# Values of three retention heads by seven products instead of eight

## The chip, the cores and the metric

The kernel runs on one core of a Trainium2 chip. The metric is the time of one execution on the device in microseconds (us). Engines go by the names of the profile: PE is TensorE's matmul, PEld its weight load, DVE is VectorE, ACT is ScalarE, POOL is GpSimd, SP is SyncE.

## The reference, cut to what matters

A trunk of two decoder layers over 512 tokens of 1024 channels, all in float32. Each layer has a half-step SwiGLU, a token mixer, a second half-step SwiGLU and a gated embedding. The mixer of the first layer is a retention with 4 heads; the change is in its input projections.

```python
def retention(h, w_in, gn_w, w_out):
    B, S, _ = h.shape                       # 1, 512 tokens
    H, DK, DV, C = RET_HEADS, RET_DK, RET_DV, RET_CHUNK     # 4, 256, 512, 128
    q, k, v, g = jnp.split(h @ w_in, [H * DK, 2 * H * DK, 2 * H * DK + H * DV], axis=-1)
    pos = jnp.arange(S, dtype=jnp.float32)
    q = rotary(q.reshape(B, S, H, DK), pos)
    k = rotary(k.reshape(B, S, H, DK), pos) * (DK ** -0.5)
    v = v.reshape(B, S, H, DV)
...
    y = jax.nn.silu(g) * o.reshape(B, S, H * DV)
    return y @ w_out
```

The values `v` are, for each head, a product of 512 tokens x 1024 channels with 1024 x 512 weights.

## The kernel before, in words

**Precision.** A float32 product is made of three products of rounded parts: each operand is split into a high part (a cast to float32r on ACT, line 88 or 134) and a low part (what the cast lost). `Weights.split` (line 86) makes the low part on DVE (line 89). `Weights.negated` makes it without DVE: ACT casts (134) and writes the negative (135), and a DMA from POOL's queue (136) reads the weights from memory once more and adds them to that negative. Pairs marked `direct` are split, the others negated.

**Seven products.** Most projections are by the Strassen-Winograd scheme: a weight block of 1024 x 256 is a `Pair` of two tensors, `q` (blocks a11 and a22) and `r` (a12 and a21). The activations' side has fixed forms (`b11`, `b22`, `b21`, `t1` to `t4`), each held as high and low part in `unit_a` to `unit_d`; the weights' side needs four sums (`sums`, line 168, on DVE), each split again into the tiles `s12` and `s34`, and the parts of a12 in the tile `a12`; the profile calls these `s` and `a`. The blocks of `q` are split in a large tile `w8`, which the profile calls `w`. `Strassen.begin` multiplies the first three products (36 matmuls of 256 columns) into two banks of PSUM, `g` and `u`, and adds across the banks (L597 to L601); `rest` does the other four (48 matmuls); `join` the last additions (L621 to L623).

**The retention's projections.** Queries and keys of heads 1, 2, 3, 0 and six gates are 14 such pairs (`ret_order`), numbered 0 to 13: 2 and 3 are head 2, 4 and 5 head 3, 6 and 7 head 0, 8 to 13 gates. The loop begins pair i + 1, then does the rest of pair i, then `finished(i)` (joins and, for a query or key, six DVE instructions of the rotary). The values of a head are plain products: `values` takes four weight chunks of 1024 columns (`ret_v`), and streams them in 96 matmuls of 512 columns with the activations as stationary operand into four banks, one for each 128 tokens (L871 to L873); ACT evicts them (L876) and POOL stores them (L877). Head 1's come ahead of the loop; `RET_V = {1: 2, 4: 3, 7: 0}` puts head 2's behind the rest of pair 1, head 3's behind pair 4, head 0's behind pair 7.

**What sets the order.** PE runs in the order in which the code is written. A scheduler sets the order on DVE, ACT, POOL and SP; each engine then works strictly in its order. `W.plan` is the order in which weights are loaded by SP into four `wraw` tiles, and `take` prepares tiles two entries ahead. There are three `w8` tiles, three each of `s12` and `s34`, two of `a12`, seven `tmp`, eight banks, each used in turn. `next_sums(behind)` makes the sums of the pair after next, ordered behind a DVE instruction.

Of the kernel before, what the change touches and what calls it, by code (L numbers as in the profile page):

```python
# [27 lines left out]
LOOKAHEAD = 2  # L28
RET_V = {1: 2, 4: 3, 7: 0}
KEPT = 7  # L30
# [27 lines left out]
class Weights:  # L58
# [149 lines left out]

    def next_sums(self, behind):
        self.pairs_used += 1  # L210
        if self.held:
            with self.tc.issue_after(behind.ins):
                self.held()
            self.held = None
        self.behind = (behind,)
        self.emit_sums()
        self.behind = ()
# [3 lines left out]
def trunk(ctx, tc, a):  # L221
# [24 lines left out]
    for i in range(4):  # L246
# [6 lines left out]
        ffn_src.append((ins, outs))  # L253
    ret_v = [[a["ret_v"][h][:, c * 1024 : (c + 1) * 1024] for c in range(4)] for h in range(RH)]
    ret_g = [[a["ret_g"][c] for c in range(4)]]
    at = {"q": 0, "k": 4, "0": 8, "1": 9}
    ret_pairs = []
    for kind, hd in ret_order:
        i = at[kind] + (hd if kind in "qk" else 2 * (hd - 1))
        ret_pairs.append(Pair(4, a["ret_p"][i, 0], a["ret_p"][i, 1]))  # L260
    for i in [0, 1] + [i + 2 for i in RET_V]:
        ret_pairs[i].direct = True
# [20 lines left out]
    plan_ffn(0)  # L283
    W.plan += ret_v[1] + ret_pairs[0:1]
    for i in range(len(ret_pairs)):
        W.plan += ret_pairs[i + 1 : i + 2]
        if i in RET_V:
            W.plan += ret_v[RET_V[i]]
    W.plan += ret_g[0] + ret_o[0] + ret_o[1] + ret_o[2][0:2]
# [41 lines left out]
    def temp(dtype=F32):  # L331
        return tmp.tile([P, S], dtype, name="tmp")
# [247 lines left out]
    class Strassen:  # L580
# [5 lines left out]
        def begin(self, pair, between=None):  # L586
            c0, c1 = HALVES
            forms = self.n.forms
            W.take(pair)
            g, u = bank(), bank()  # L590
            product(g[:, c0], pair.t[0], 0, forms, "b11", True)
            if between:
                between()
            product(g[:, c1], pair.s[0], 0, forms, "t1")
            product(u[:, c1], pair.s[1], 0, forms, "t2", True)
            cc = temp()
            nc.scalar.copy(cc, g)  # L597
            nc.vector.tensor_tensor(out=u[:, c1], in0=u[:, c1], in1=cc[:, c0], op=ALU.add)
            u2 = temp()[:, c0]
            nc.scalar.copy(u2, u[:, c1])  # L600
            last = nc.vector.tensor_tensor(out=g[:, c1], in0=g[:, c1], in1=u2, op=ALU.add)  # L601
            self.live[id(pair)] = g, u, cc
            W.next_sums(last)

# [11 lines left out]
        def join(self, pair):  # L616

            c0, c1 = HALVES
            g, u, cc = self.live.pop(id(pair))
            u3 = temp()[:, c0]  # L620
            nc.scalar.copy(u3, u[:, c1])  # L621
            nc.vector.tensor_tensor(out=u[:, c1], in0=u[:, c1], in1=cc[:, c1], op=ALU.add)
            nc.vector.tensor_tensor(out=u[:, c0], in0=u[:, c0], in1=u3, op=ALU.add)  # L623
            return g, u

    def ffn(i, n, nxt, stack, apool, meanwhile=None):
# [198 lines left out]
    def retention(n, nxt, pools):  # L825
        stack, hold, sums = pools
        kept = [dram.tile([P, 2, S], F32, name=f"kept{i}") for i in range(28)]
        qd, kd = kept[0:4], kept[4:8]
        vd = [kept[8 + 2 * i : 10 + 2 * i] for i in range(RH)]
        gd = [kept[16 + 2 * i : 18 + 2 * i] for i in range(RH)]  # L830
        slot = lambda i: stat.tile([P, S], F32, name="acc") if i else hold.tile([P, S], F32, name="slot")
# [28 lines left out]

        def values(hd, to):
            os = [bank() for _ in range(NT)]
            for c in range(4):
                wh, wl = W.take(ret_v[hd][c])
                for j in range(2):
# [8 lines left out]
            for t in range(NT):  # L874
                t1 = temp()
                nc.scalar.copy(t1, os[t])  # L876
                nc.gpsimd.dma_start(out=to[t // 2][:, t % 2, :], in_=t1)  # L877

# [20 lines left out]
        def finished(i):  # L899
# [4 lines left out]
            else:  # L904
                gates(*x, gd[hd][int(kind)])

        W.begin(())
        values(1, vd[1])
        by7.begin(ret_pairs[0])
# [3 lines left out]
        for i in range(len(ret_pairs)):  # L913
            if i + 1 < len(ret_pairs):
                by7.begin(ret_pairs[i + 1])
            by7.rest(ret_pairs[i])
            finished(i)
            if i == 0:
                n.rows()
            if i in RET_V:  # L920
                values(RET_V[i], vd[RET_V[i]])
            if ret_order[i] == ("k", 0):
                decay(0)
                decay(1)
# [623 lines left out]
def _layout(x, p, norm_w, ffn_w_in, ffn_w_out, ret_w_in, ret_gn_w, ret_w_out,  # L1548
# [8 lines left out]
    def quarters(t):  # L1557


        t = t.reshape(2, -1, P, KB // 2, 2, P).transpose(1, 0, 4, 2, 3, 5).reshape(-1, 2, 2, P, 512)  # L1560
        return np.stack(
            [np.concatenate([t[:, 0, 0], t[:, 1, 1]], axis=2), np.concatenate([t[:, 0, 1], t[:, 1, 0]], axis=2)],
            axis=1,
        )

    def wide(w):
# [4 lines left out]
    def outp(w):  # L1571
# [24 lines left out]
        "ret_p": quarters(np.concatenate([tiles(rw[:, :2048]), tiles(rw[:, 4608:])]).reshape(14, 2, P, D).transpose(1, 0, 2, 3)),  # L1596
        "ret_v": c(wide(rw[:, 2048:4096])),
        "ret_g": c(tiles(rw[:, 4096:4608])),
# [30 lines left out]
```

## Time and profile before

| | |
|---|---|
| median of 3 runs | 2111.88 us (2110.74 to 2112.08) |
| the profiled execution | 2111.21 us; span of its instructions 2109.4 us |
| chain that ended last | PE 89%; DVE 4% |
| DMA | 304.16 MB, mean 144 GB/s |

The profile is of one execution. Busy shares tell how much an engine did, not whether anyone waited for it. The chain goes back from the last instruction, at each step to what released it. Matmuls are pipelined, so the mean duration of one is longer than the distance between two starts; the distance is read from the chain, where a run of matmuls has its length and count. Lines are those of the kernel before.

### The profile page before, as it was taken

To read this page: it belongs to the slowest core of one execution; us is meant where nothing else is said; L and a number is where in the kernel's file an instruction comes from. 1 tells how busy PE (TensorE), PEld (TensorE's weight loads), DVE (VectorE), ACT (ScalarE), POOL (GpSimd) and SP (SyncE) were. 2 spreads that over 40 slices of the span, in tenths; PEclk is the share of its full clock that TensorE was granted. 3 is DMA by queue.
4 is the path that set the end of the run, shared out by engine and by line. 5 is a ranking of instruction groups with operands and counts; after the bars stand their busy time and mean duration, and the time that the engine had idled before them with its cause. 6 is when DMAs were issued, how large, how long until landed. Compare 5 with 4: busy or idle time off the path is not lost.

```text
span 2109.4 us, 36167 instructions
## 1 busy us (share of the span) xinstructions
PE 2096.1 (99%) x14089; PEld 1925.6 (91%) x14089; DVE 1581.1 (75%) x2943; ACT 1287.4 (61%) x2225; POOL 276.9 (13%) x292
## 2 busy tenths in 40 slices
PE   9999999999999999999999999999999999999998
PEld 9999998999998898989889999998888899999988
DVE  9786769677767887868768786766675687877775
ACT  8474556555665673737467465555796784655555
POOL 0010100121200010101001010110334210101100
PEclk9999999999999999999999999999999999999999
DMA  6475554666777374737435575553322355755631
GB/s 194 122 181 135 151 140 130 186 193 182 233 212 180 100 180 119 196 111 171 122 117 141 127 181 138 146 149 110 111 89 72 110 133 128 173 148 145 160 110 41
DMA packets 108492, 304.16 MB, mean 144 GB/s; under 512 B 11280, under 2 KB 14864, under 8 KB 108320
## 3 DMA queue, kind: packets, MB, share of 16 engines
q1 hardware_dynamic: 65088, 212.92, 30.7%
q0 software_dynamic: 38544, 81.54, 21.5%
q10 hardware_dynamic: 4688, 7.39, 1.0%
q8 instruction: 110, 1.80, 0.3%
q14 instruction: 62, 0.51, 0.1%
HBM read 289.19 MB, written 12.62 MB: 143 GB/s over the span
## 4 chain that ended last, share of the span: by engine, by line
PE 89%; DVE 4%; issue 2%; ACT 2%; DMA 2%; POOL 0%; SPq 0%; POOLq 0%; ACTq 0%; DVEq 0%
PE bank L570 42%; PE bank L354 12%; PE bank L353 12%; PE bank L355 12%; PE bank L651 2%; DMA wraw<-in_ffn_w_in 1%; PE bank L555 1%; PE bank L871 1%; PE bank L872 1%; PE bank L873 1%; PE bank L805 1%; PE bank L806 1%; PE bank L807 1%; PE bank L1256 1%; ACT p L1239 0%
## 5 line engine op out<-in xcount | busy, mean ns | idle before, releaser
L88 ACT CAST w<-wraw 128x1024 fp32r<-128x1024 f32 (+1 forms) x198 | 199.9, 1016 | 296.2 <-PE bank L355 203.7
L570 PE MATMUL bank<-unit_a,s 128*128 128x256 f32 x2229 | 326.9, 276 | 0.0
L89 DVE TENSOR_TENSOR s<-sums,s 128x512 fp32r<-128x512 f32 x380 | 251.4, 686 | 100.8 <-ACT s L88 99.9
L88 ACT CAST s<-sums 128x512 fp32r<-128x512 f32 x380 | 224.6, 618 | 163.5 <-PE bank L570 76.0
L570 PEld LDWEIGHTS bank<-unit_a,s 128*128 128x128 f32 x2229 | 288.5, 188 | 0.0
L353 PE MATMUL bank<-unit_d,w 128*128 128x512 f32 x656 | 255.6, 390 | 0.3 <-DVE tmp L1273 0.3
L354 PE MATMUL bank<-unit_d,w 128*128 128x512 f32 x656 | 255.3, 389 | 0.0
L355 PE MATMUL bank<-unit_d,w 128*128 128x512 f32 x656 | 255.2, 389 | 0.0
L89 DVE TENSOR_TENSOR w<-wraw,w 128x1024 fp32r<-128x1024 f32 (+1 forms) x176 | 206.0, 1171 | 34.6 <-ACT w L88 34.0
L570 PE MATMUL bank<-unit_b,s 128*128 128x256 f32 x1064 | 226.3, 277 | 1.8 <-ACT s L88 1.8
L353 PE MATMUL bank<-unit_a,w 128*128 128x512 f32 (+1 forms) x536 | 199.1, 371 | 0.0
L354 PE MATMUL bank<-unit_a,w 128*128 128x512 f32 (+1 forms) x536 | 198.2, 370 | 0.0
L355 PE MATMUL bank<-unit_a,w 128*128 128x512 f32 (+1 forms) x536 | 198.2, 370 | 0.0
L680 DVE SCALAR_TENSOR_TENSOR tmp<-bank,rows 128x512 f32<-128x512 f32 x96 | 66.1, 689 | 144.9 <-PE bank L355 144.8
L570 PEld LDWEIGHTS bank<-unit_b,s 128*128 128x128 f32 x1064 | 169.3, 188 | 2.0 <-ACT s L88 2.0
L570 PE MATMUL bank<-unit_b,w 128*128 128x256 f32 x855 | 156.9, 281 | 0.5 <-DMA w<-in_ret_p 0.3
L570 PE MATMUL bank<-unit_c,s 128*128 128x256 f32 x700 | 153.3, 276 | 0.0
L570 PE MATMUL bank<-unit_a,w 128*128 128x256 f32 x993 | 152.0, 278 | 0.0
L353 PEld LDWEIGHTS bank<-unit_d,w 128*128 128x128 f32 x656 | 123.1, 188 | 25.8 <-DVE tmp L1273 0.5
L136 POOL DMA_DIRECT2D a<-in_ffn_w_in x82 | 72.2, 881 | 566.9 <-ACT a L135 429.9
L355 PEld LDWEIGHTS bank<-unit_d,w 128*128 128x128 f32 x656 | 123.2, 188 | 25.7
L354 PEld LDWEIGHTS bank<-unit_d,w 128*128 128x128 f32 x656 | 123.2, 188 | 25.2
(356 smaller groups left out, 4827.1 us busy)
## 6 DMA issues: line engine op xcount, KB each, us to landing
wraw<-in_ffn_w_in SPq DMA_DIRECT2D x174, 512.0 KB, 4.6
wraw<-in_ffn_w_out SPq DMA_DIRECT2D x64, 512.0 KB, 4.5
w<-in_ffn_w_in POOLq DMA_DIRECT2D x63, 512.0 KB, 5.6
a<-in_ffn_w_in POOLq DMA_DIRECT2D x81, 256.0 KB, 6.3
wraw<-in_ret_p SPq DMA_DIRECT2D x28, 512.0 KB, 3.5
wraw<-in_ffn_w_out SPq DMA_DIRECT2D x32, 384.0 KB, 3.5
kept<-tmp POOLq DMA_DIRECT2D x40, 256.0 KB, 3.6
wraw<-in_ret_v SPq DMA_DIRECT2D x16, 512.0 KB, 4.9
```

The source lines that it names most:

```text
L88: self.cast = self.nc.scalar.copy(hi, raw)
L89: low.tensor_tensor(out=lo, in0=raw, in1=hi.bitcast(F32), op=ALU.subtract)
L136: self.nc.gpsimd.dma_start(out=lo, in_=src, accum_op=ALU.add)
L353: nc.tensor.matmul(out, wh, xh, start=first, stop=False)
L354: nc.tensor.matmul(out, wh, xl, start=False, stop=False)
L355: nc.tensor.matmul(out, wl, xh, start=False, stop=last)
L555: nc.tensor.matmul(o[:, half], w[:, ks], x, start=k == t == q == 0, stop=k == KB - 1 and q == 2, skip_group_check=True,)
L570: add = lambda w, x, start, stop: nc.tensor.matmul(out, w, x, start=start, stop=stop, skip_group_check=True)
L651: nc.tensor.matmul(o[:, HALVES[t]], x[:, ks], y, start=k == t == q == 0, stop=k == KB - 1 and q == 2, skip_group_check=True,)
L680: nc.vector.scalar_tensor_tensor(out=t1, in0=o, scalar=-0.5, in1=n.r, op0=ALU.mult, op1=ALU.mult)
L805: nc.tensor.matmul(os[t], xh, wh[:, js], start=k == 0, stop=False)
L806: nc.tensor.matmul(os[t], xh, wl[:, js], start=False, stop=False)
```

## The change

Values of heads 2, 3 and 0 are made by seven products, with the weights now in the streaming place and the activations' forms stationary. A new class `StrassenValues` cuts a head's weights into two pairs, one for each half of the 1024 channels (`ret_v7`), and the tokens into two blocks of each half, so four banks are filled: `begin_half` does three products of one pair (36 matmuls of 256 columns), `rest_half` four (48). Both halves' first products are done together, ahead of the rest of the pair at hand; behind that rest, the next pair is begun, and then the rest of both halves is done, joined, evicted by ACT (L931 of the kernel after) and stored. The copies of the banks that the joins use go to free `unit_d` tiles. `RET_V` now names pairs 1, 3 and 5, so head 0's queries and keys (pairs 6 and 7) and then the gates come behind the last values. Head 1's values stay as they were. The pairs split directly are now 0, 1, 2, 4 and 6 (before 0, 1, 3, 6 and 9).

```diff
-RET_V = {1: 2, 4: 3, 7: 0}
+RET_V = {1: 2, 3: 3, 5: 0}
...
-    def next_sums(self, behind):
+    def next_sums(self, behind=None):
         self.pairs_used += 1
...
-        self.behind = (behind,)
+        self.behind = (behind,) if behind else ()
         self.emit_sums()
...
-    for i in [0, 1] + [i + 2 for i in RET_V]:
+    for i in [0, 1] + [i + 1 for i in RET_V]:
         ret_pairs[i].direct = True
...
-    W.plan += ret_v[1] + ret_pairs[0:1]
-    for i in range(len(ret_pairs)):
-        W.plan += ret_pairs[i + 1 : i + 2]
+    W.plan += ret_v1
+    for i, pair in enumerate(ret_pairs):
+        W.plan.append(pair)
         if i in RET_V:
-            W.plan += ret_v[RET_V[i]]
+            W.plan += ret_v7[RET_V[i]]
...
+    class StrassenValues(Strassen):
+        def part(self, out, w, c, j, r, name, first=False):
+            ts_ = slice(r * P, (r + 1) * P)
+            add = lambda x, w, start, stop: nc.tensor.matmul(out, x, w, start=start, stop=stop, skip_group_check=True)
+            for i in range(2):
+                xh, xl = (x[:, ts_] for x in self.n.forms[2 * j + i][name])
+                wh, wl = (w[:, s, c + i * H2 : c + (i + 1) * H2] for s in range(2))
+                add(xh, wh, first and j == i == 0, False)
+                add(xh, wl, False, False)
+                add(xl, wh, False, j == i == 1)
+
+        def begin_half(self, pairs, j):
+            c0, c1 = HALVES
+            if j == 0:
+                self.banks = [(bank(), bank()) for _ in range(2)]
+            pair = pairs[j]
+            W.take(pair)
+            for w, at, name in ((pair.t[0], (0, c0), "b11"), (pair.s[0], (0, c1), "t1"), (pair.s[1], (1, c1), "t2")):
+                for r, gu in enumerate(self.banks):
+                    self.part(gu[at[0]][:, at[1]], w, 0, j, r, name, name != "t1")
+            if j:
+                self.copies, last = zip(*(self.shared(*gu, unit(ud).bitcast(F32)) for gu in self.banks))
+                W.next_sums(last[1])
+            else:
+                W.next_sums()
+
+        def rest_half(self, pairs, j):
+            c0, c1 = HALVES
+            pair = pairs[j]
+            for w, at, name in (
+                (pair.t[1], (1, c0), "t4"), (pair.s[3], (0, c1), "b22"), (pair.s[2], (1, c1), "t3"), (pair.x, (0, c0), "b21")
+            ):
+                for r, gu in enumerate(self.banks):
+                    self.part(gu[at[0]][:, at[1]], w, 0, j, r, name)
...
         for i in range(len(ret_pairs)):
-            if i + 1 < len(ret_pairs):
+            head = RET_V.get(i)
+            if head is not None:
+                v7.begin_half(ret_v7[head], 0)
+                v7.begin_half(ret_v7[head], 1)
+            elif i + 1 < len(ret_pairs):
                 by7.begin(ret_pairs[i + 1])
             by7.rest(ret_pairs[i])
             finished(i)
...
-            if i in RET_V:
-                values(RET_V[i], vd[RET_V[i]])
+            if head is not None:
+                by7.begin(ret_pairs[i + 1])
+                v7.rest_half(ret_v7[head], 0)
+                v7.rest_half(ret_v7[head], 1)
+                keep_values(v7.tiles(), vkept[head])
```

`shared` and `joined` are the additions that `begin` and `join` had before, now for use by both classes. `keep_values` evicts the four tiles with ACT and stores each with one DMA of 256 rows of 256.

How the order changes is shown for head 0. PE before: the start of its values, which stream a chunk `w_5…` through stationary `unit` tiles (the second name), behind pair 7.

```order
L871 MATMUL bank<-w_5569,unit_b 128x512
L872 MATMUL bank<-w_5569,unit_b 128x512
L873 MATMUL bank<-w_5569,unit_b 128x512
L871 MATMUL bank<-w_5569,unit_b 128x512
L872 MATMUL bank<-w_5569,unit_b 128x512
```

PE after: the end of the first half's beginning, the whole beginning of the second half, and the first product of pair 5's rest. `w_5553` is the second half's large tile.

```order
L637 MATMUL bank<-s_5416,unit_c 128x256 x3
L637 MATMUL bank<-w_5553,unit_a 128x256 x12
L637 MATMUL bank<-s_5607,unit_a 128x256 x12
L637 MATMUL bank<-s_5608,unit_a 128x256 x12
L571 MATMUL bank<-unit_b,w_5217 128x256 x2
L571 MATMUL bank<-unit_a,w_5217 128x256 x6
```

The values' matmuls are half as wide, and stand between the beginning of pair 5 and its rest.

ACT, which prepares those tiles. Before, around a head's evictions (L876), with the large tiles of the next two pairs (`w_5306` split, `w_5361` negated):

```order
L88 CAST s_5371<-sums 128x512
L88 CAST w_5306<-wraw 128x2x512
L876 COPY tmp<-bank 128x512 x3
L134 CAST w_5361<-wraw 128x2x512
L135 ACTIVATE w_5361<-wraw 128x2x512
L876 COPY tmp<-bank 128x512
L88 CAST s_5372<-sums 128x512
```

After, around head 3's evictions (L931) and head 0's second half:

```order
L931 ACTIVATE tmp<-bank 128x512
L88 CAST s_5415<-sums 128x512
L134 CAST a_5279<-wraw 128x512
L135 ACTIVATE a_5279<-wraw 128x512
L88 CAST s_5416<-sums 128x512
L931 ACTIVATE tmp<-bank 128x512 x3
L603 COPY tmp<-bank 128x512
L134 CAST w_5553<-wraw 128x2x512
L135 ACTIVATE w_5553<-wraw 128x2x512
L88 CAST s_5277<-sums 128x512
```

Three evictions and the copy of pair 5's bank (L603) now stand ahead of the cast of `w_5553`, which takes the buffer that `w_5150` (pair 4) had.

More of the change, by code (lines that the diff above doesn't have):

```diff
@@ L253, in trunk @@
         ffn_src.append((ins, outs))
-    ret_v = [[a["ret_v"][h][:, c * 1024 : (c + 1) * 1024] for c in range(4)] for h in range(RH)]
+    ret_v1 = [a["ret_v1"][:, c * 1024 : (c + 1) * 1024] for c in range(4)]
+    ret_v7 = {h: [Pair(4, a["ret_v7"][i, j, 0], a["ret_v7"][i, j, 1]) for j in range(2)] for i, h in enumerate((0, 2, 3))}
     ret_g = [[a["ret_g"][c] for c in range(4)]]
@@ L595, in begin, with shared @@
             product(u[:, c1], pair.s[1], 0, forms, "t2", True)
-            cc = temp()
+            cc, last = self.shared(g, u, temp())
+            self.live[id(pair)] = g, u, cc
+            W.next_sums(last)
+        def shared(self, g, u, cc):
+            c0, c1 = HALVES
             nc.scalar.copy(cc, g)
@@ L600, in begin @@
             nc.scalar.copy(u2, u[:, c1])
-            last = nc.vector.tensor_tensor(out=g[:, c1], in0=g[:, c1], in1=u2, op=ALU.add)
-            self.live[id(pair)] = g, u, cc
-            W.next_sums(last)
+            return cc, nc.vector.tensor_tensor(out=g[:, c1], in0=g[:, c1], in1=u2, op=ALU.add)
         def rest(self, pair, between=None):
@@ L616, in join, with joined @@
         def join(self, pair):
+            return self.joined(*self.live.pop(id(pair)))
+        def joined(self, g, u, cc):
             c0, c1 = HALVES
-            g, u, cc = self.live.pop(id(pair))
             u3 = temp()[:, c0]
@@ L624, in join, with tiles @@
             return g, u
+    class StrassenValues(Strassen):
[23 more added lines that the diff above has]
+        def rest_half(self, pairs, j):
+            c0, c1 = HALVES
+            pair = pairs[j]
[4 more added lines that the diff above has]
+                    self.part(gu[at[0]][:, at[1]], w, 0, j, r, name)
+        def tiles(self):
+            return [self.joined(*gu, cc) for gu, cc in zip(self.banks, self.copies)]
     def ffn(i, n, nxt, stack, apool, meanwhile=None):
@@ L826, in retention @@
         stack, hold, sums = pools
-        kept = [dram.tile([P, 2, S], F32, name=f"kept{i}") for i in range(28)]
+        kept = [dram.tile([P, 2, S], F32, name=f"kept{i}") for i in range(16)]
         qd, kd = kept[0:4], kept[4:8]
-        vd = [kept[8 + 2 * i : 10 + 2 * i] for i in range(RH)]
-        gd = [kept[16 + 2 * i : 18 + 2 * i] for i in range(RH)]
+        gd = [kept[8 + 2 * i : 10 + 2 * i] for i in range(RH)]
+        vkept = [dram.tile([P, 2, 2, S], F32, name=f"values{i}") for i in range(RH)]
+        vd = [[t[:, i] for i in range(2)] for t in vkept]
         slot = lambda i: stat.tile([P, S], F32, name="acc") if i else hold.tile([P, S], F32, name="slot")
@@ L859, in gates, with values @@
                 nc.gpsimd.dma_start(out=to[:, s, :], in_=t1)
-        def values(hd, to):
+        def values(to):
             os = [bank() for _ in range(NT)]
             for c in range(4):
-                wh, wl = W.take(ret_v[hd][c])
+                wh, wl = W.take(ret_v1[c])
                 for j in range(2):
@@ L876, in values, with keep_values @@
                 nc.scalar.copy(t1, os[t])
-                nc.gpsimd.dma_start(out=to[t // 2][:, t % 2, :], in_=t1)
+                nc.gpsimd.dma_start(out=to[:, t // 2, t % 2, :], in_=t1)
+        def keep_values(tiles, to):
+            for r, gu in enumerate(tiles):
+                for s, x in enumerate(gu):
+                    t1 = temp()
+                    nc.scalar.mul(t1, x, 1.0 - 2 * s)
+                    nc.gpsimd.dma_start(
+                        out=to[:, :, r, s * H2 : (s + 1) * H2], in_=t1.rearrange("p (h f) -> p h f", h=2)
+                    )
         def fetch(src, low=ud, high=ud, queue=nc.scalar):
@@ L905, in finished @@
                 gates(*x, gd[hd][int(kind)])
+        v7 = StrassenValues(n)
         W.begin(())
-        values(1, vd[1])
+        values(vkept[1])
         by7.begin(ret_pairs[0])
@@ L1560, in quarters, with crossed @@
         t = t.reshape(2, -1, P, KB // 2, 2, P).transpose(1, 0, 4, 2, 3, 5).reshape(-1, 2, 2, P, 512)
+        return crossed(t)
+    def crossed(t):
         return np.stack(
@@ L1564, in quarters, with values @@
         )
+    def values(w):
+        return crossed(w.reshape(2, 2, 2, P, 2, H2).transpose(0, 4, 2, 3, 1, 5).reshape(2, 2, 2, P, 512))
     def wide(w):
@@ L1596, in _layout @@
         "ret_p": quarters(np.concatenate([tiles(rw[:, :2048]), tiles(rw[:, 4608:])]).reshape(14, 2, P, D).transpose(1, 0, 2, 3)),
-        "ret_v": c(wide(rw[:, 2048:4096])),
+        "ret_v1": c(wide(rw[:, 2560:3072])[0]),
+        "ret_v7": np.stack([values(rw[:, 2048 + 512 * i : 2560 + 512 * i]) for i in (0, 2, 3)]),
         "ret_g": c(tiles(rw[:, 4096:4608])),
```

## The prediction

> **What bounds the kernel now.** I read the page's busy shares first, then its chain, then the stretches of the retention's projections, then who waited for whom in them. In the first row the numbers are busy time, share and instructions; in the second the share of the chain by engine.
>
> ```profile
> PE 2096.1 (99%) x14089; PEld 1925.6 (91%) x14089; DVE 1581.1 (75%) x2943; ACT 1287.4 (61%) x2225; POOL 276.9 (13%) x292
> PE 89%; DVE 4%; issue 2%; ACT 2%; DMA 2%; POOL 0%; SPq 0%; POOLq 0%; ACTq 0%; DVEq 0%
> ```
>
> TensorE holds the end. The stretch that the change touches runs from 368.4 us (first product of the first retention pair) to 569.9 us. Columns: stretch, length, busy time and instructions of PE, PEld, DVE, ACT, POOL, granted clock, DMA share, GB/s. The second and third rows are one period of today's loop each (three pairs, then one head's values); the first is 20 us inside the third.
>
> ```profile
> 480.00:500.00 20.00, 20.00 (x150) 18.92 (x149) 19.63 (x34) 11.78 (x21) 2.92 (x4) 1.00 0.66 186
> 392.50:443.20 50.70, 50.70 (x351) 46.93 (x350) 36.37 (x60) 25.23 (x40) 10.51 (x15) 1.00 0.69 193
> 443.20:493.80 50.60, 50.60 (x350) 46.84 (x349) 37.28 (x62) 26.48 (x42) 9.36 (x13) 1.00 0.65 181
> 368.40:569.90 201.50, 201.24 (x1472) 189.66 (x1471) 142.45 (x243) 113.50 (x186) 42.26 (x60) 1.00 0.71 199
> ```
>
> TensorE is busy for 201.24 of 201.50 us at full clock, so work taken from it shortens the stretch, and any wait put in front of it lengthens it. VectorE is at 71% of the stretch, yet at 98% in the first row: it works in bursts. Of all the waits of TensorE from 360 to 620 us these two were listed:
>
> ```profile
> PE bank L354 <- DVE ulo L344: 0.4, 1, 0.4
> PE bank L570 <- DMA w<-in_ret_p: 0.3, 1, 0.3
> ```
>
> The second is the one to remember: a weight tile `w` that came late through GpSimd's DMA queue.
>
> **TensorE's own work.** From the chain in order of time (start, length, what): the first and last listed of the 96 matmuls of 512 columns of a head's values, the 252 of 256 columns behind them, a later run of 256-column matmuls of another line, and one that followed the wait.
>
> ```profile
> 392.67 0.23 PE bank L871
> ...
> 414.00 0.23 PE bank L872
> 414.45 28.80 PE bank L570 x252
> ...
> 518.00 8.38 DMA w<-in_ret_p
> 526.43 43.45 PE bank L570 x376
> 573.65 5.81 PE bank L555 x48
> ```
>
> A head's values take 414.45 - 392.67 = 21.78 us, so three take 65.3. Seven products need per head 2 halves x 7 x 2 token blocks x 2 k blocks x 3 = 168 matmuls of 256 columns, 504 in all. The rows give two paces: 28.80/252 = 114.3 ns (mostly the small sum tiles) and 5.81/48 = 121.0 ns (large `w` tiles). I take 121 ns for the 72 that stream the first quarter of a large tile and 114.3 for the other 432, which is the mix that L570 has: 8.7 + 49.4 = 58.1 us. TensorE saves 7.2 us; the ends are 65.3 - 57.6 = 7.7 (all at 114.3) and 65.3 - 61.0 = 4.3 (all at 121).
>
> [...]
>
> **What the other engines get.** Rows of VectorE and ScalarE in 368 to 530 us (busy, then mean ns of one):
>
> ```profile
> L89 DVE TENSOR_TENSOR s<-sums,s 128x512 fp32r<-128x512 f32 x40 | 26.9, 686 | 28.9 <-ACT s L88 28.8
> L89 DVE TENSOR_TENSOR w<-wraw,w 128x1024 fp32r<-128x1024 f32 x15 | 18.3, 1223 | 11.0 <-ACT w L88 10.9
> L168 DVE TENSOR_TENSOR sums<-sums,wraw 128x512 f32<-128x512 f32 x20 | 13.7, 684 | 0.1
> L598 DVE TENSOR_TENSOR bank<-bank,tmp 128x256 f32<-128x256 f32 x10 | 4.3, 427 | 0.3
> L88 ACT CAST s<-sums 128x512 fp32r<-128x512 f32 x40 | 24.2, 619 | 22.4 <-DVE sums L168 14.0 <-PE bank L570 6.9 <-ACT s L88 1.4
> L876 ACT COPY tmp<-bank 128x512 f32<-128x512 f32 x14 | 8.1, 585 | 7.5 <-PE bank L873 6.9
> L135 ACT ACTIVATE w<-wraw 128x1024 fp32r<-128x1024 f32 x7 | 7.4, 1060 | 0.0
> L134 ACT CAST w<-wraw 128x1024 fp32r<-128x1024 f32 x7 | 7.4, 1052 | 1.8 <-PE bank L570 1.3
> L135 ACT ACTIVATE a<-wraw 128x512 fp32r<-128x512 f32 x9 | 5.7, 631 | 0.0
> L600 ACT COPY tmp<-bank 128x256 f32<-128x256 f32 x10 | 3.7, 373 | 7.6 <-DVE bank L598 7.6
> ```
>
> VectorE, per head: four low parts of 1024 go (4 x 1.22 = 4.9 us); eight sums (0.684), eight low parts (0.686) and eight additions in the banks (0.427) come, 14.4. Net +9.5, three heads +28.5: 171 of some 194 us, 88%. In the new period (two pairs and a head, 2 x 9.6 + 19.4 = 38.6 us of TensorE) stand 61 VectorE instructions; at 36.37/60 = 0.606 us each that is 37.0 us, under TensorE's time but by 1.6 us only. I cost it at nothing; its cover is gone where one takes 0.63 us on the mean.
>
> ScalarE, per head: four casts of 1.05 go and the four evictions stay; two casts with their negations (2.11 each), eight small casts, two pairs on the 512-wide tiles (about 1.25) and six copies (two of 0.585, four of 0.373) come: 14.3 - 4.2 = +10.1, in all 144 of 194 us, 74%. GpSimd gets four more accumulating DMAs per head, 1.57 MB; the stretch moves about 40 MB today, so 4.7 MB more lift the DMA share from 0.71 to some 0.82. SyncE loads the same four 512 KB chunks per head. The values go out in runs half as long (256x1x256 for 128x512); I price that at nothing, since nobody reads them for tens of us.
>
> Pairs 6 and 7 now have no values behind them: 20 VectorE instructions each, 12.1 us at 0.606, against 9.6 of TensorE. The 2.5 us each are covered: their banks are taken again only four pairs later, and the sums that VectorE would then be late with belong to a pair whose first product is a full pair, 9.6 us, away. Without that lead the 5 us would stand on the path. The gates behind have 14 instructions each and give it back.
>
> **The new wait.** The three large `w` buffers go round. The second half of a head's values takes the buffer of the pair in the middle of the cycle (w_5553 that of w_5150), which is free after the 12th matmul of that pair's rest. From there TensorE has 36 matmuls of the rest and 36 of the first half's beginning, 72 x 114.3 ns = 8.2 us, until it needs the second half's. In that time ScalarE must cast and negate (2.1 us), and GpSimd's DMA must land. Landings of such tiles in 365 to 550 us, and the page's row of the whole kernel:
>
> ```profile
> DMA to landing us min/median/max: 5.5/6.5/8.4
> w<-in_ffn_w_in POOLq DMA_DIRECT2D x63, 512.0 KB, 5.6
> ```
>
> So 7.6 us at the least, 8.6 at the median, 10.5 at the most. In ScalarE's order three evictions of the head before and a copy of a bank stand right ahead of that cast, and these evictions wait for VectorE's joins: 4 x 0.585 = 2.3 us in a row, of which I count 1.0 as delay. The low part is read by the second matmul already. That gives 9.6 - 8.2 = 1.4 us of wait for each head, 4.3 in all; the ends are 0 and 3 x (10.5 + 2.3 - 8.2) = 13.8. Queued behind that cast on ScalarE are the small casts that VectorE's next low parts want, so the delay is passed on there; behind the tile's DMA on GpSimd waits the 512-wide one, not needed for another 20 us.
>
> [...]
>
> Room elsewhere: the pair right behind the first products is cast without a DMA (1.05 + 1.22 us in the 36 matmuls, 4.1 us, hidden); the next has 84 matmuls, 9.6 us, against 8.6, hidden at the median. The run behind the wait of 518 us took 43.45/376 = 115.6 ns a matmul, not 114.3: 0.5 us. I add 0.5 for three such runs in place of today's one.
>
> **Sum.** -7.2 + 4.3 + 0.5 = -2.4 us. The profiled execution took 2111.21 us (span 2109.4); the median of the runs is 2111.88, 0.03% above. On the median: 2109.5 us. About 0.2%, 4.2 us, is what a measurement of this kernel tells from no change: faster is below 2107.7, slower above 2116.1.
>
> **Rivals.** (1) No wait: ScalarE gets to the cast at once and the tiles land in 5.5 to 6 us as the faster half did. -7.2 us, 2104.7; for it speaks that before had 0.3 us of such waits in all, against it that today's second tile has more room. Chance 0.31.
> (2) Slower: the second half's tile lands late at the top of the rows in every cycle, 4.6 us three times: -7.2 + 13.8 + 0.5 = +7.1, 2119.0. It decides from 3.6 us per head. For it speak the DMA share that rises and landings of 7 to 8 us right behind the evictions' writes; against it, that TensorE's wait itself lets ScalarE catch up. Chance 0.14.
> (3) VectorE becomes the bound: with no overlap of neighbours the cycle's 45 instructions of 512 or more columns (one of them 1.22 us, the rest 0.685) and 16 of 256 take 38.2 us, still under 38.6; its waits for ScalarE's casts, 28.8 us for 40 low parts today, must then leave 1.5 us in a cycle: 39.7, so +1.1 three times, and the wait of the forecast besides: -7.2 + 3.3 + 4.8 = +0.9, 2112.8. The first of the four rows above (34 instructions in 20 us, 0.58 each) speaks against it. Chance 0.08.
> (4) The change doesn't give its saving: all 504 at 121 ns, -4.3 + 4.8 = +0.5, 2112.4. Chance 0.06.
> The weight-load rule would give 2111.9 + 11.7, 2123.6, which the half pace at 256 columns leaves at 0.01. The forecast holds 0.40.
>
> **Numbers.** Faster: rival 1 and a tenth of the forecast's cases, 0.35. Slower: rival 2, the rule, and a little of 3, 0.17. The rest, 0.48, within 0.2%. The range leaves out a tenth at each end: 2104.4 (just below rival 1) to 2117.0 (into rival 2). The forecast alone would run from 2107 to 2113.
>
> **What would show it.** Right: the values' matmuls at 114 to 116 ns in the chain, three waits of TensorE for a `w` from the values' tensor of 1 to 2 us, VectorE near 88% of the stretch, which ends 2 us sooner after its start. Wrong: no such wait (rival 1), waits of 4 us (2), TensorE waiting for `s` tiles or banks from VectorE (3), 120 ns (4).

## The result, and the profile after

The changed kernel takes 2124.01 us (median of 4 runs, 2120.63 to 2126.60) against 2111.68 for the kernel before: 1.0056 of its time, 95% interval 1.0044 to 1.0068. It is slower by 12 us, where the prediction had 2109.5 in a range of 2104.4 to 2117.0. The profiled execution took 2126.22 us, its span is 2124.4. In four of the experiments below one execution was slow (2297 to 5413 us); the medians count it, the ratios leave it out.

The page of after, busy time and the chain by engine:

```profile
PE 2096.3 (99%) x14305; PEld 1936.0 (91%) x14305; DVE 1604.2 (76%) x3003; ACT 1312.6 (62%) x2279; POOL 291.9 (14%) x304
PE 84%; DVE 6%; ACT 4%; DMA 3%; issue 2%; POOL 0%; SPq 0%; POOLq 0%; ACTq 0%; DVEq 0%
```

TensorE's busy time is what it was (2096.1 before), and DMA, VectorE and ScalarE have a larger part of the chain: TensorE was spared work, and waits came. The same stretch as before (from the first product of the first pair to the first one behind the last pair; same columns):

```profile
369.20:581.40 212.20, 200.34 (x1687) 199.06 (x1687) 165.33 (x304) 138.19 (x240) 56.13 (x72) 0.98 0.79 211
```

And the waits of TensorE in 360 to 620 us (us in total, times, longest):

```profile
PE bank L637 <- DMA w<-in_ret_v: 10.0, 3, 4.9
PE bank L571 <- ACT tmp L606: 1.9, 3, 0.8
```

212.20 us stand against 201.50, so 10.7 us longer. TensorE is busy for 200.34 of them against 201.24, and waits for 11.9, all of it in the two rows: three times for the large tile of a head's second half, three times, in the rest of pairs 8, 9 and 10 (the first gates, right behind pairs 6 and 7), for the copy of a bank. The second surprise is that the busy time fell by 0.9 us only, with 7 us less to compute. Stretches of after around the two longest waits show why (the last three columns are the granted clock, the DMA share and GB/s):

```profile
410.00:420.00 10.00, 10.00 (x88) 10.00 (x87) 6.92 (x13) 7.34 (x14) 3.62 (x4) 1.00 0.99 220
420.00:430.00 10.00, 8.31 (x73) 8.11 (x71) 6.72 (x16) 7.94 (x14) 4.23 (x5) 1.00 0.96 285
432.00:438.00 6.00, 4.77 (x24) 4.77 (x25) 3.86 (x7) 0.59 (x1) 1.16 (x2) 0.54 0.72 235
438.00:440.00 2.00, 2.00 (x20) 2.00 (x19) 1.09 (x3) 1.48 (x3) 0.00 (x0) 1.00 0.17 66
478.00:482.00 4.00, 3.76 (x19) 3.77 (x20) 4.00 (x8) 0.00 (x0) 0.58 (x1) 0.57 0.97 310
```

Behind the wait that ends at 433 us the granted clock is 0.54, and 24 matmuls take 4.77 us, 199 ns each; from 438 on 20 take 2.00. In the trace 18 of them are 213 ns apart, and 16 behind the wait that ends at 478, 3.4 us too long together. Two smaller terms are the first matmul behind each wait (some 225 ns) and the mean distance of all the others: 117 ns for the values' matmuls, where the forecast had 115.3 (58.1/504), and 115.1 for the pairs', where before had 114.4. They come to 0.8 and 1.7. So -7.2 + 3.4 + 0.8 + 1.7 = -1.3, near the -0.9 of the rows.

Of the profiled execution's 15.0 us more, 10.7 are in this stretch; 0.8 come ahead of it, in the first 10 us; 2.2 at one wait near 760 us, in the feed-forward behind the retention; and 1.3 behind the last piece of the chain, at the program's end. Another execution of the same kernel (below) has the first and the last of these four, not the two in the middle.

### The profile page after: what moved, and what is told of

The parts are those of the page before. It is cut to its first block, busy times and chain, and to the rows that moved or that the text cites. A ratio compares the mean times of both kernels' runs of the same rounds, so it can differ in the third digit from the quotient of the medians.

```text
span 2124.4 us, 36761 instructions
## 1 busy us (share of the span) xinstructions
PE 2096.3 (99%) x14305; PEld 1936.0 (91%) x14305; DVE 1604.2 (76%) x3003; ACT 1312.6 (62%) x2279; POOL 291.9 (14%) x304
## 4 chain that ended last, share of the span: by engine, by line
PE 84%; DVE 6%; ACT 4%; DMA 3%; issue 2%; POOL 0%; SPq 0%; POOLq 0%; ACTq 0%; DVEq 0%
PE bank L571 38%; PE bank L355 12%; PE bank L354 12%; PE bank L356 12%; PE bank L697 2%; DMA wraw<-in_ffn_w_in 1%; PE bank L556 1%; DMA w<-in_ret_v 1%; DVE sums L168 1%; DMA wraw<-in_ret_p 1%; PE bank L637 1%; DVE s L89 1%; PE bank L851 1%; PE bank L853 1%; PE bank L852 1%
## 5 line engine op out<-in xcount | busy, mean ns | idle before, releaser
L88 ACT CAST w<-wraw 128x1024 fp32r<-128x1024 f32 (+1 forms) x186 | 187.2, 1014 | 280.6 <-PE bank L356 200.8
L88 ACT CAST s<-sums 128x512 fp32r<-128x512 f32 x404 | 239.9, 618 | 178.0 <-DVE sums L168 85.2
L89 DVE TENSOR_TENSOR s<-sums,s 128x512 fp32r<-128x512 f32 x404 | 268.4, 686 | 79.6 <-ACT s L88 78.8
L89 DVE TENSOR_TENSOR w<-wraw,w 128x1024 fp32r<-128x1024 f32 (+1 forms) x164 | 191.2, 1168 | 27.2 <-ACT w L88 26.9
L168 DVE TENSOR_TENSOR sums<-wraw 128x512 f32<-128x512 f32 x202 | 138.2, 685 | 19.7 <-DMA wraw<-in_ffn_w_in 11.4
L356 PEld LDWEIGHTS bank<-unit_d,w 128*128 128x128 f32 x656 | 123.1, 188 | 25.8
L354 PEld LDWEIGHTS bank<-unit_d,w 128*128 128x128 f32 x656 | 123.2, 188 | 25.8 <-DVE tmp L1338 0.5
```

What stands on the lines that cost most here:

```text
L88: self.cast = self.nc.scalar.copy(hi, raw)
L89: low.tensor_tensor(out=lo, in0=raw, in1=hi.bitcast(F32), op=ALU.subtract)
L168: add = lambda o, p, q: nc.vector.tensor_tensor(out=o, in0=p, in1=q, op=ALU.add)
L354: nc.tensor.matmul(out, wh, xh, start=first, stop=False)
L356: nc.tensor.matmul(out, wl, xh, start=False, stop=last)
```

## The experiments

The theory after the result (A): the second half's tile comes too late for the 8.2 us of room that it has, and the waits are long enough to take the clock down as well. The rival (B): VectorE and ScalarE are too slow for the new cycle, and the tile's wait is where it happens to show. The kernel before was timed beside each group, at medians of 2112.6 to 2114.0.

| kernel | median us | ratio to before (95%) |
|---|---|---|
| again (the change) | 2126.22 | 1.0054 (1.0042 to 1.0066) |
| filler | 2122.08 | 1.0042 (1.0030 to 1.0054) |
| apart | 2121.20 | 1.0035 (1.0023 to 1.0047) |
| direct | 2121.34 | 1.0036 (1.0024 to 1.0048) |
| early | 2133.86 | 1.0095 (1.0082 to 1.0108) |
| early2 | 2144.09 | 1.0139 (1.0126 to 1.0153) |
| placed | 2113.38 | 0.9999 (0.9990 to 1.0007) |
| mid | 2116.89 | 1.0021 (1.0012 to 1.0029) |
| spread | 2117.83 | 1.0021 (1.0013 to 1.0029) |
| spread_long | 2117.50 | 1.0020 (1.0011 to 1.0030) |
| spread_half | 2112.13 | 0.9994 (0.9984 to 1.0003) |
| spread_half_long | 2112.24 | 0.9998 (0.9989 to 1.0008) |
| spread_mid | 2111.48 | 0.9996 (0.9986 to 1.0007) |
| spread_mid_half | 2112.99 | 1.0001 (0.9992 to 1.0010) |
| spread_mid_act | 2112.81 | 1.0003 (0.9994 to 1.0012) |
| spread_kept | 2116.85 | 1.0017 (1.0008 to 1.0026) |
| spread_mid_kept | 2114.66 | 1.0006 (0.9997 to 1.0015) |

### The change again, and work in place of the waits

> The changed kernel once more, unchanged. Theory A (the second half's large tile lands too late): TensorE waits three times for a weight tile of the values' tensor, 1.4, 5.1 and 4.2 us in the profile at hand (10.6 in all), and behind the two long waits some 24 matmuls run at 164 to 174 ns instead of 114 to 118; all of it is there again, and the time is 2120.6 to 2126.6 us. The wait of 2.3 us for an s tile near 760 us, in the feed-forward behind the retention, is either there again (then the change causes it) or absent (then it belongs to single executions and splits the times of 2121 from those of 2126). Rival B (VectorE and ScalarE are the bound, the tile's wait is a symptom): the waits wander between w and s tiles from run to run.

The waits are the same ones in the same places (8.8 us for the tile, 2.5 for the banks), which is against a wandering bound. The wait near 760 us was not there, so not every execution of the change has it. Waits of 0.8 to 2.6 us near that place are in five of the later variants' traces, though, and in none of before and placed: whether the change favours them is open.

```diff
-            for w, at, name in ((pair.t[0], (0, c0), "b11"), ...):
+            for w, at, name in (2 - j) * ((pair.t[0], (0, c0), "b11"), ...):   # begin_half
```

> The first half's 36 first products are computed twice in a row (the second pass starts their sums anew), which puts 4.1 us of TensorE work in front of the second half's first product in each of three heads, 12.3 us of additional work in all. Theory A: the work falls into the waits, which become 0, 1.0 and 0.1 us, and with no long wait the slow matmuls behind (3.4 us) go: 2124.0 + 12.3 - 9.6 - 3.4 = 2123.3 us (2121 to 2126), so the same time with 108 more matmuls. Theory A without a clock effect: 2126.7. Rival B: the waits are set by the other engines' pace, which more room in one place does not mend: up to 2136 us.

108 more matmuls, 12.3 us of work, and the time is no longer than the change's on the same chip (4 us less, with intervals that overlap); 2122 lies in A's range with the clock effect, 2121 to 2126. One row of TensorE's waits above 0.4 us is left in the stretch, none is for the tile, and no matmuls behind a wait are slow:

```profile
PE bank L571 <- ACT tmp L606: 1.9, 3, 0.8
```

The added work gives the other engines 12 us more as well, so B isn't out by this run alone. Its chain gives the values' matmuls undisturbed, 118 ns each:

```profile
490.61 5.67 PE bank L637 x48
```

### More room, or no landing

```diff
             if head is not None:            # apart
                 v7.begin_half(ret_v7[head], 0)
-                v7.begin_half(ret_v7[head], 1)
...
             by7.rest(ret_pairs[i])
...
+                v7.begin_half(ret_v7[head], 1)
                 by7.begin(ret_pairs[i + 1])
...
+    for p in ret_v7.values():               # direct
+        p[1].direct = True
```

> The second half's first products stand behind the pair's remaining products instead of right behind the first half's: 48 more matmuls (5.5 us) between the matmul that frees the large tile's buffer and the first that needs the tile, so 13.7 us of room instead of 8.2. Theory A: the three waits (10.6 us) and the slow matmuls behind them (about 3.4 us) go, 2124.0 - 14 = 2110 us (2108 to 2112), a little faster than before the change. Rival B (VectorE and ScalarE are too slow for this cycle): the waits move to s tiles and banks, at most 4 us come back, 2120 us.

> The order stays, but the second half's large tile gets its low part from VectorE (1.2 us each, three more) instead of the negation on ScalarE and the accumulating DMA. Theory A: the landing of 7.6 us falls away, the tile is there about 5.5 us after its buffer is free against 7.7 us of room; waits and slow matmuls go, 2110 us (2108 to 2113). Rival B: VectorE has 3.7 us more to do in the very stretch that it bounds, so no gain, 2122 to 2126 us. Rival C (GpSimd's queue is what is late): the next tiles on that queue gain as well, which is as A in the time.

A's 2110 is missed by both: 5 us came back, not 14, and B's figures (2120 for apart, 2122 to 2126 for direct) are nearer. TensorE's longest waits in apart:

```profile
PE bank L637 <- ACT tmp L606: 7.5, 5, 3.3
```

And in direct:

```profile
PE bank L637 <- DVE s L89: 3.1, 5, 1.1
PE bank L571 <- ACT tmp L606: 2.7, 3, 1.3
PE bank L571 <- DMA w<-in_ret_p: 1.8, 2, 0.9
```

No wait for the values' tile is left, so A is right on what made that wait, not on what its going is worth. Apart puts the second half's first products only 36 matmuls ahead of the halves' rest, whose banks must first be combined by ScalarE and VectorE; that was hidden behind 84 matmuls. Direct shows B's part: VectorE's own tiles come late.

So the room had to be found elsewhere. Mid calls `begin_half` of the second half between the two halves of the pair's rest: 24 matmuls more of room, 24 fewer in front of the banks.

```diff
-                v7.begin_half(ret_v7[head], 1)
+                between = lambda: v7.begin_half(ret_v7[head], 1)
...
-            by7.rest(ret_pairs[i])
+            by7.rest(ret_pairs[i], between if head is not None else None)
```

> The changed kernel with its own places (behind pairs 1, 3 and 5), and the second half's first products in the middle of the pair's rest, 2.7 us more of room for its large tile. Theory A (the tile's room alone made the loss): waits for it of 0, 2.4 and 1.5 us instead of 1.4, 5.1 and 4.2, no slow matmuls; -6.8 - 3.4 = 10 us under the changed kernel's 2124 to 2126: 2115 us. Rival F (the close places leave VectorE no slack, so that other waits fill the gap as in the kernels apart and direct): 2120 us or more.

2116.9, some 7 to 9 us below the change and nearer to A's 2115 than to F's 2120: more room alone mends most of the loss. Its longest waits:

```profile
PE bank L637 <- DMA w<-in_ret_v: 3.3, 2, 2.0
PE bank L571 <- DMA w<-in_ret_p: 1.7, 2, 1.3
```

A run of the values' matmuls in its chain, and the stretch behind the longest wait:

```profile
382.87 4.18 PE bank L637 x36
```

```profile
464.90:468.70 3.80, 3.79 (x19) 3.79 (x20) 1.84 (x5) 2.29 (x6) 0.23 (x1) 0.56 1.07 336
```

Of the change's three waits for a second half's tile one is left, with 1.3 us. The 2.0 are for another tile, that of the first half of head 0's values: it was issued at 453.97 and landed 10.9 us later, where the change's slowest took 9.0. Behind that wait the clock is 0.56 again, which A had not expected.

Early and early2 looked for the room in another way, freeing a tile's buffer sooner by another order of products.

```diff
             product(g[:, c0], pair.t[0], 0, forms, "b11", True)
+            product(u[:, c0], pair.t[1], 0, forms, "t4", True)      # was the first of rest
```

> The retention pairs' product with the large tile's second quarter (t4) is taken from the rest to the pair's first products, right behind the product with the first quarter; nothing is added or left out. A pair's large tile is then free 24 matmuls after the pair begins, so the second half's cast stands in ScalarE's order ahead of three of the four evictions. Theory A (the late tile costs 10.6 us of waits and 3.4 us of slow matmuls behind them): both go, 14 us below the changed kernel of the same chip (2126 there, so 2112; 2 us faster than before's 2114). Rival B (VectorE and ScalarE bound the cycle, and only the 12 us of additional work in the filler let them keep up): the waits move to s tiles and banks as they did where VectorE split the tile, 2120 us.

> As the kernel early, and the values' halves too take their t4 products among the first products (48 matmuls in a row on each half's large tile). Theory A: the second half's tile is needed 24 matmuls (2.7 us) later still, so no wait for it, 2112 us as early; if early still shows waits of 1 to 2 us for it, they are gone here. Rival B: 2120 us.

Both are 8 to 18 us slower than the change, which neither theory had. Early's waits for the tile are 4.3 us, but there is a new one, for the joins on VectorE:

```profile
PE bank L571 <- DVE bank L609: 10.2, 4, 6.1
```

The edit made the scheduler put a cast ahead of evictions, and the orders of VectorE and GpSimd differ from there on; which of these makes the joins late was not tried.

### The places

```diff
-RET_V = {1: 2, 3: 3, 5: 0}
+RET_V = {1: 2, 4: 3, 7: 0}     # spread; placed is the reverse, in the kernel before
```

> Seven products, but for the heads' old places in the order (behind pairs 1, 4 and 7 instead of 1, 3 and 5). Theory A: the three waits for the values' large tile stay (10 us), the three waits of the last two pairs for a bank's copy (0.9, 0.7, 1.0 us) go, 3 us below the changed kernel. Rival D (the places are what costs): VectorE has a pair more per period, the tile comes in time, 2114 us or less.

> The kernel before with only the three heads' places changed (behind pairs 1, 3 and 5), values by eight plain products. Theory A: only the last two pairs' waits come, +2.5 to +3 us on before. Rival D (places): +8 us or more. If the places cost nothing: 0.

Placed costs nothing (0.9999); the 2.5 us expected for the last two pairs are not there with plain values. Yet the same places are worth 6 to 8 us with seven products: more than A's 3 us, but short of D's 2114 or less. Spread's only waits in the stretch above 0.4 us:

```profile
PE bank L637 <- DMA w<-in_ret_v: 6.2, 3, 2.8
```

The waits for a bank's copy are gone, and those for the tile are 6.2 us instead of 10.0. This trace is of the fastest of spread's twelve executions, 2113.15 us. Head 0's queries and keys without values behind them, and cycles of two pairs rather than three, cost only together with what seven products add; which part of that (VectorE's work, ScalarE's, the DMAs) was not tried.

### What makes the tile late

Four runs worked on spread. Half gives the first quarter of the second half's tile to VectorE (half of direct's work) and leaves the second quarter, whose first read comes some 20 us later (168 matmuls, not the 9.6 us of the expectation), to the DMA; long writes the values out in rows of 2 KB.

```diff
+        if pair.half:
+            self.split(pair.raw[:, 0:512], hi[:, 0, :], lo[:, 0, :])
+            self.negated(pair.raw[:, 512:1024], hi[:, 1, :], lo[:, 1, :], pair.q[:, 512:1024])
...
-                    nc.gpsimd.dma_start(out=to[:, :, r, s * H2 : (s + 1) * H2], in_=t1.rearrange("p (h f) -> p h f", h=2))
+                    nc.gpsimd.dma_start(out=to[:, r, s, :], in_=t1)      # long
```

> The kernel spread, with the first quarter of the second half's large tile (that which its first products read) split by ScalarE and VectorE from the loaded chunk (0.6 us each), and only the second quarter, which is read 9.6 us later, filled by the negation and GpSimd's DMA. Spread's profile has 7.0 us of waits for this tile and 1.6 us of slow matmuls behind one of them. Theory A (the DMA's landing is what is late): both go, 2117.8 - 8.6 = 2109 us (2108 to 2112), faster than before's 2113.4. Rival B (VectorE is at its limit, other waits take the place as in the kernel direct): 2114 to 2118 us.

> The kernel spread, with the second half's first products moved into the middle of the pair's rest: 24 matmuls (2.7 us) more of room for its large tile, 24 fewer between its first products and the halves' rest. Theory A: the waits for the tile go from 1.1, 3.0 and 2.9 us to 0, 0.3 and 0.2, no slow matmuls; the room in front of the halves' rest is 6.9 us where apart needed 6 to 8, so at most 1 us of wait there per head: 2109 to 2113 us. Rival B: 2115 us or more.

> The kernel spread, with the values of the three heads written out in rows of 2 KB (128x512) instead of two runs of 1 KB (256x1x256); the reads of them, much later, take the short runs instead. If the short runs slow the tiles' landings (rival E; the values' writes land in 5.1 to 7.6 us, those of the kept queries in 2.7), the writes land in 3 to 4 us, the tile's DMA behind them some 0.5 to 1 us sooner, 2115 us. If they do nothing (as the prediction costed them): 2117.8 us.

> Both edits of spread_half and spread_long together. Theory A: 2109 us, as spread_half, or 1 us less if the long runs help the other tiles too. Rival B: as spread_half, 2114 us or more.

Without the DMA in front of the first product, or with 2.7 us more of room, the time falls by 6 us, to that of the kernel before. For spread_mid that is in A's range; for spread_half A gave 8.6, read from spread's fast trace and taken off its median, and B's lower bound was 2114. The tile's wait is gone from spread_half's trace, but some for `s` tiles are left:

```profile
PE bank L642 <- ACT s L88: 1.8, 2, 1.3
PE bank L642 <- DVE s L89: 1.0, 2, 0.5
```

The length of the runs does nothing for the time, with half (2112.24 against 2112.13) or without (2117.50 against 2117.83). Spread_mid's trace, taken in a second execution (2113.83 us):

> The kernel spread_mid once more, for its profile. Theory A: no wait for the values' large tile above 0.3 us, no matmuls at 213 ns, at most 1 us of wait per head in front of the halves' rest, and the stretch of the retention's projections ends 3 us or more sooner than before the change; GpSimd's drain at the end 5.9 us.

```profile
PE bank L571 <- DMA w<-in_ret_p: 2.0, 2, 1.2
PE bank L637 <- DMA w<-in_ret_v: 0.5, 1, 0.5
PE bank L637 <- ACT tmp L606: 0.4, 1, 0.4
```

The wait for the values' tile is nearly gone and the clock stays up, as expected. The size is not: the stretch, to the first product behind the last pair, is 1.5 us shorter than before, not 3.

> The edits of spread_mid and spread_half together. Theory A: each alone already takes the waits for the large tile, so together nothing more: 2111 to 2112 us; the waits that spread_half has left (4 us for s tiles of the second half's first products, which come 2.7 us later here) go: 2109 us. Rival B (VectorE): 2112 us or more.

Together they give nothing more, which fits A's first case: what each takes away is the same wait. But 2113.0 is also in B's range (2112 or more), and this trace has 3.1 us of waits for a bank's copy, so the run doesn't part the two.

In spread, ScalarE had done its part in time, and GpSimd's queue was held for 5.3 us (from 427.78) by a write of rotated keys. The last two runs gave those writes to SyncE.

```diff
-                    nc.gpsimd.dma_start(out=to[:, s, :], in_=t1)     # rotate
+                    nc.sync.dma_start(out=to[:, s, :], in_=t1)
```

> The kernel spread, with the twelve writes of rotated queries and keys (L898) issued from SyncE's queue instead of GpSimd's. In spread's trace ScalarE's negation for the second half's tile ends at 430.4 us, but its DMA starts at 433.6, behind a write of rotated keys that held GpSimd's queue for 5.3 us until VectorE's rotation. Theory H (the in-order queue of GpSimd is what makes the tile late there): the DMA starts 3 us sooner, the waits fall from 1.1, 3.0 and 2.9 us to 1.1, 0 and 0, no slow matmuls, and GpSimd's drain at the end is about 1 us shorter: 2117.8 - 7.5 - 1 = 2109 us. Theory A alone (the landing, whatever stands ahead): the waits stay, 2116.5. Rival: the writes hold up SyncE's loads instead, waits for s tiles, 2114 us or more.

> The kernel spread_mid with the same twelve writes on SyncE's queue. Its trace has no wait above 0.5 us for the values' tile, but 2.0 us for the pairs' tiles. Theory H: these go too, and the end's drain is about 1 us shorter: 2111.5 - 3 = 2108.5 us, 0.2% faster than before the change. If only the drain gains: 2110.5. Rival: SyncE's loads are held up, 2113 us or more.

Theory H falls: 2116.85 is A's 2116.5, not 2109. Its failure is the best reading of the study. From the chain of spread, and 10 us around it:

```profile
433.64 5.80 DMA w<-in_ret_v
```

```profile
430.00:440.00 10.00, 7.25 (x63) 7.05 (x62) 9.97 (x19) 4.74 (x10) 3.13 (x4) 1.00 0.96 255
```

The same of spread_kept:

```profile
430.62 8.22 DMA w<-in_ret_v
```

```profile
430.00:440.00 10.00, 7.76 (x67) 7.56 (x66) 9.96 (x19) 4.65 (x10) 1.97 (x2) 1.00 1.04 279
```

The DMA was issued 3.0 us sooner and landed 0.6 sooner (438.84 instead of 439.44), because it took 8.22 us instead of 5.80. The DMA engines' share is about 1 here, as in the 20 us ahead of the change's longest wait: the transfer that was issued sooner into full DMA engines took longer there, by most of what it had gained. The third head's tile did the same: issued 3.5 us sooner, it took 7.98 us instead of 5.64 and landed 1.2 sooner. No wait for an `s` tile is listed in spread_kept, so SyncE's loads were not what held it up. Which of the other transfers slowed the tile was not tried. In spread_mid_kept a pair's tile still has a wait of 1.9 us; its 2114.66 us are in the rival's range, not in H's.

### The end of the program

> The kernel spread_mid with the twelve value writes of the three heads issued from ScalarE's queue, behind the eviction that makes them, instead of GpSimd's. At the end of the program GpSimd's last drain takes 4.2 us before the change and 5.9 with it. Theory G (this drain grows with what GpSimd's software queue has carried): it falls to 4.9 us or so, 1 us; and the weight tiles' DMAs, no more behind these writes, land sooner: 2111.5 - 1 to 2 = 2110 us. Otherwise the drain stays at 5.9, and the issues on ScalarE (0.4 us each) cost up to 1 us: 2111.5 to 2113.

The chain's last piece in the kernel before:

```profile
2104.84 0.69 POOL hall L1476
```

In the changed kernel:

```profile
2118.48 0.68 POOL hall L1541
```

And in spread_mid_act:

```profile
2108.49 0.68 POOL hall L1541
```

The spans are 2109.4, 2124.4 and 2113.3, so 3.9, 5.2 and 4.1 us follow. In the trace this is GpSimd's last drain: 4.2, 5.9 and 4.8 us. Theory G's number for the drain is met. The median is not lower (2112.81 against 2111.48, in different groups, with ratios whose intervals overlap): TensorE's waits in the stretch are 5.2 us here and 3.1 in spread_mid_b.

## Why the prediction was wrong

**TensorE's saving, -7.2: nearly right.** The values' matmuls run at 116 ns (4.18/36 in mid) and 118 (5.67/48 in filler), forecast 114 to 116. In the change's own trace they are 117 ns apart on the mean, without those at half clock and those behind a wait: 504 take 59.0 us, so 6.3 are saved. No run shows the 11.7 us more of the weight-load rule that I left at 0.01: in the traces the pace is 227 ns at 512 columns (21.78/96 before) and 116 to 118 at 256, about half. That its 2123.6 lies next to the measured 2124.0 is a coincidence of two numbers.

**The new wait, 1.4 us per head: the failed step.** It is the right wait on the right tile, but it is 1.1, 4.9 and 4.0 us (the row above has the sum and the longest). The mis-sized term is the delay in ScalarE's order, "of which I count 1.0 as delay". The second wait, first in the chain of after:

```profile
410.69 5.51 DMA wraw<-in_ret_v
...
425.44 7.75 DMA w<-in_ret_v
```

And in its timeline of VectorE and ScalarE (start, length, what; in brackets the idle time and who ended it):

```profile
416.33 0.69 DVE L168 TENSOR_TENSOR sums<-wraw 128x512 f32<-128x512 f32 x1 [2.01 <-DMA wraw<-in_ret_v]
419.95 0.76 DVE L628 TENSOR_TENSOR bank<-bank,unit_d 128x256 f32<-128x256 f32 x2
421.07 1.59 ACT L931 ACTIVATE tmp<-bank 128x512 f32<-128x512 f32 x3 [1.83 <-DVE bank L629]
423.13 1.05 ACT L134 CAST w<-wraw 128x1024 fp32r<-128x1024 f32 x1
```

A raw chunk is issued at 410.69, when a `wraw` tile came free, and lands at 416.20. VectorE stands for 2.0 us waiting for it, with the joins of the head before behind those sums in its order; in the trace TensorE had finished that head at 414.4. So the joins come at 419.95, the evictions at 421.07, and the cast behind them at 423.13. The stalled matmul's place in time, 428.0, less 72 matmuls puts the buffer's release at about 419.8: 3.3 us of delay, not 1.0. Cast and negation to the issue take 2.3 (2.1 forecast), and the landing 7.75 (6.5). Together 13.4 us against 8.2 of room. The third wait has 3.8 and a landing of 6.27; the first, which has no evictions ahead of its cast, 1.4 and 5.87. I counted the evictions' own 2.3 us in part, and not what they in turn wait for. The waits of 10.0 us in place of 4.3 are the largest part of the error. That the evictions' wait made the delay is read from the trace; no run moved the evictions alone.

**The landing, 6.5 us.** The six tiles of the values landed in 5.9 to 9.0. I set the DMA share at a mean of 0.82 (it is 0.79 over the stretch). From issue to landing of the three second halves' tiles it is 0.75, 0.93 and 0.88, and these landings take 5.87, 7.75 and 6.27 us. The fastest of the tiles that GpSimd's DMA adds to landed in 5.5 us, the fastest plain load of 512 KB in this stretch, into `wraw`, in 3.5.

**What a long wait costs besides: missing.** Rival 2, late tiles at 4.6 us each, was the nearest of those worked out from rows, at 2119.0. Its waits are too long (13.8 us against 10.0), by a landing at the top of the rows instead of a late cast, and it has no clock in it: 3.4 us of half-speed matmuls.

**Pairs 6 and 7 "covered": wrong by 1.9 us** in three waits. I looked at when their banks are taken again and at the sums. What came late is the exchange between the two banks of pairs 8 to 10, ahead of their rest, behind VectorE's work for pairs 6 and 7. Two rows of after's stretches, same columns as above:

```profile
520.00:530.00 10.00, 9.34 (x81) 9.14 (x81) 9.96 (x19) 6.53 (x12) 1.97 (x2) 1.00 1.02 226
530.00:540.00 10.00, 9.54 (x80) 9.34 (x80) 9.62 (x19) 7.50 (x13) 1.98 (x2) 1.00 0.83 192
```

**VectorE at 88%:** 165.33 of 212.20 us, 78%; even of 201.5 us it would be 82%. It is not the bound by its sum, but it is full where it counts, as the row of direct and the two rows here show. ScalarE has 138 us, forecast 144. The value writes at nothing: right, as spread_long shows for spread.

**The end, costed at nothing:** +1.3 us, a resource that I did not look at.

Together: -7.2 + 10.0 + 1.9 + 3.4 + 0.8 + 1.7 + 1.3 = +11.9, where the medians have +12.3. The 1.7 hold the values' slower pace, the 0.8 the first matmul behind each wait.

## What to carry to other kernels

A new wait is sized from the moment the buffer is free to the landing, and the queue ahead of the cast counts with what its instructions themselves wait for, not with their durations. DMA shares are read in the 10 us in which the tile must move, not over the stretch; where the share was near 1, an earlier issue bought little here (0.6 of 3.0 us), and more room, or a tile filled without a DMA, took the wait away. Seven products save TensorE 6.3 us here, and the versions with the fewest waits (spread_half, spread_mid and those built on them) end within 0.1% of the eight plain products. In spread_mid_b's trace the stretch keeps 1.5 of the 6.3 us, and the longer end takes 1.3 of these: with TensorE at 99% busy, what feeding it cost decided here.

## What the runs showed of the hardware that I had not expected

**Behind some waits the granted clock was halved.** In the change's trace the waits for the values' tile are, from start to start of two matmuls, 1.38 us (from 387.83), 5.20 (from 428.04) and 4.24 (from 474.00). Behind the first the next matmuls run at their usual pace. Behind the second and the third they are 213 to 214 ns apart (the values' matmuls otherwise mostly 113 to 120), and the records of the granted clock have it at half from 430.65 to 437.48 and from 478.44 to 481.85 us.

Other runs, with the waits of the lists above: in mid the clock is 0.56 behind a wait of 2.0 us. In early, whose longest wait is 6.1 us, it is 0.66 in the 10 us from 530, in which TensorE is busy for 4.47. In direct (longest wait 1.3) and filler (0.8) it is 1.00 in every 10 us from 390 to 560. In spread the second of the tile's waits is 2.8 us, and the clock stays at 1.00 in the 10 us around it (430 to 440) and in the 10 us behind (440 to 450); behind the third, which is no longer, it is 0.83 (490 to 500). So the length of a wait alone does not tell whether the clock falls; what decides was not settled.

**GpSimd's last drain took longer in the changed kernel.** It takes 4.2 us before, and 5.9 with twelve more accumulating DMAs and twelve value writes of twice the runs on its queue. In spread_mid_act, without the twelve writes, it takes 4.8. In spread_kept, without the twelve writes of the rotated queries and keys, 4.9 us follow the chain's last piece, against 3.9 before and 5.2 in the changed kernel. What it counts was not settled.
